# q and k split behind whole transposes, one exponential per row, one search for five blocks, junk as bytes

## The chip, the cores and the metric

The kernel runs on one core of one Trainium2 chip. The metric is the device time of one execution in microseconds (us); smaller is better. Five engines work side by side, each with its own queue that it takes in order: TensorE (PE; PEld is its weight load), VectorE (DVE), ScalarE (ACT), GpSimd (POOL) and SyncE (SP), which here only issues DMAs.

## The reference

One layer of a hybrid decoder: x is (1, 1024, 1024) float32. After an RMSNorm one projection gives everything that two attention branches of eight heads (64 wide) need. Branch A attends, for each query, to the 256 causal keys with the highest score of a light indexer; branch B to dilated windows. Cut to what the change touches:

```python
qa = rms_norm(qa.reshape(b, s, N_HEADS_A, HEAD_DIM), q_norm_a[layer])   # k, and branch B, likewise
rel = jnp.einsum('bqhd,bsd->bqhs', qib, k_idx)                          # indexer, 4 heads
score = jnp.einsum('bqhs,bqh->bqs', jax.nn.relu(rel), wb) * idx_scale
score = jnp.where(causal[None], score, -jnp.inf)
top_val, top_idx = lax.top_k(score, topk)                               # topk = 256
logits = jnp.einsum('bqhd,bqkhd->bqhk', qb, k_sel) * scale + bias
p = jax.nn.softmax(logits, axis=-1)
out = jnp.einsum('bqhk,bqkhd->bqhd', p, v_sel)
x = x + jnp.einsum('bse,ed->bsd', mixed * silu(gates), w_out[layer])
```

## The kernel before

The 1024 positions are eight blocks of 128. The 16 heads are eight **pairs** of two, taken one after the other: `ORDER` puts the four pairs of branch B first (pairs 0 to 3) and those of branch A last (pairs 4 to 7). Operands are kept as a high part of type fp32r and a low part, the rest, so that two or three fp32r matmuls stand for one exact product.

A list of timed steps sets the order in which the program is written: 64 **units** (pair, group s of 256 queries from s=3 down to 0, head h) have a slot each. In slot k stand the scores of unit k+1 (`scores`), the transposes and value matmuls of unit k (`pt`, `pv`), the projection of the next pair (`proj_item`), and a share of the two **searches** named in `CFG["sel"]`. A scheduler then places the steps on the engines' queues: a step that is ready may come ahead of one that was written earlier but isn't, and one that needs a buffer of a pool waits for a free one.

- **Projection** (L416 to L418): three matmuls for each of eight slices, two PSUM buffers. `finish` and `finish2` normalise q and k (L448, L456, L462), split k into two halves that lie side by side (L458, L459); `later` transposes these (four fp32r transposes, L471, for 256 keys) and one copy writes `kst` (L475).
- **q**: `split_q` splits q in the same way (L502, L503) for 256 queries; `transpose_q` makes two groups of four fp32r transposes (L512, L513) with a copy each (L515). `pk`, `pq` and the gate's `pg` share one PSUM buffer (tag `tr`).
- **Scores** (L537, L538): chunks of up to 512 keys; VectorE adds the bias and keeps the running maximum (L544, a custom operation and a read of its result); one exponential for each chunk (L554). The rows L live in a ring of six buffers of 512.
- **Probabilities**: transposed in f32 (L571), split by ScalarE (L575) and VectorE (L576), multiplied with the values (L587, L589). `make_gate` sums the denominators, `combine` joins and gates the result (L615 to L623).
- **Search**: the top 256 are found as a threshold, bit by bit. For one bit VectorE counts, for each block, the scores above a trial threshold (L260, whose element output `jk` is junk and takes a buffer of the ring L) and updates all thresholds (L267, L269). One such search serves blocks 2 and 3, one blocks 4 to 6; block 7 is counted by ScalarE (L309) with small updates on VectorE (L313, L315). At the end `select_mask` turns the scores into masks (L244 to L248), which the scores of branch A (pairs 4 to 7) need.

## Time and profile before

| | |
|---|---|
| median of 3 runs | 822.93 us (819.94 to 825.45) |
| profiled execution | 821.55 us |
| its span in the trace | 819.7 us, so 1.85 us lie outside |
| TensorE busy | 770.4 us, 94% |
| VectorE busy | 627.0 us, 76% |
| ScalarE busy | 525.0 us, 64% |
| GpSimd busy | 434.2 us, 53% |

Busy time is the time in which an engine had an instruction under way; shares are over the whole span, which is made of stages with different limits. TensorE's instructions overlap, so that the distance between two starts says more than the length of one. A stretch of the span is read by itself, with the wait that ends last there.

### The profile page before, as it was taken

How to read it: one execution, taken by the hardware profiler on the slowest of the kernel's cores; microseconds unless marked ns; L12 is line 12 of the kernel's file. 1: busy time of each engine (PE TensorE's matmuls, PEld its weight loads, DVE VectorE, ACT ScalarE, POOL GpSimd, SP SyncE). 2: the span in 40 equal slices, each digit the busy share in tenths (PEclk: the TensorE clock that was granted, in tenths of full speed). 3: DMA queues.
4: the chain of work that ended last, by engine and by line, in shares of the span. 5: the costliest groups of instructions: out<-in, count | busy, mean ns of one | idle time of the engine just before them, and what ended most of it. 6: DMA issues, size and time to landing. Idle time of an engine off the chain costs nothing.

```text
span 819.7 us, 13162 instructions
## 1 busy us (share of the span) xinstructions
PE 770.4 (94%) x4300; PEld 653.6 (80%) x4300; DVE 627.0 (76%) x1586; ACT 525.0 (64%) x1220; POOL 434.2 (53%) x452
## 2 busy tenths in 40 slices
...
GB/s 291 242 216 296 42 0 168 13 1 78 116 14 14 90 91 14 14 90 92 14 14 103 78 14 7 64 123 14 14 115 123 63 61 194 226 102 174 228 234 219
DMA packets 52053, 83.33 MB, mean 102 GB/s; under 512 B 5633, under 2 KB 23313, under 8 KB 51985
## 3 DMA queue, kind: packets, MB, share of 16 engines
...
q8 instruction: 34, 0.56, 0.3%
q14 instruction: 35, 0.28, 0.1%
...
## 4 chain that ended last, share of the span: by engine, by line
PE 59%; DVE 14%; ACT 3%; DMA 2%; issue 2%; POOL 1%; SPq 0%; DVEq 0%; POOLq 0%; ACTq 0%
PE pp L416 9%; PE pp L418 9%; PE pp L417 9%; PE pt L571 7%; PE po L589 6%; PE sp L537 4%; PE sp L538 4%; PE pp L644 3%; PE pp L646 3%; PE pp L645 3%; DVE jk L260 3%; DVE ptl L576 2%; DVE jk L245 1%; DVE L L544 1%; PE po L587 1%
## 5 line engine op out<-in xcount | busy, mean ns | idle before, releaser
L416 PE MATMUL pp<-wh,xh 128*128 128x512 f32 x512 | 210.0, 413 | 2.4 <-ACT praw L424 1.2
L417 PE MATMUL pp<-wl,xh 128*128 128x512 f32 x512 | 202.6, 396 | 2.6 <-POOL wl L85 2.5
L418 PE MATMUL pp<-wh,xl 128*128 128x512 f32 x512 | 202.3, 395 | 0.0
L554 ACT ACTIVATE L<-L,mn 128x512 f32<-128x512 f32 (+1 forms) x192 | 117.6, 615 | 54.0 <-DVE mn L544 52.2
L260 DVE TENSOR_SCALAR_CACHE_REDUCE jk<-sc,thr 128x512 bf16<-128x512 f32 (+4 forms) x160 | 136.3, 873 | 2.5 <-PE pt L571 2.2
L85 POOL TENSOR_TENSOR wl<-raw,wh 128x512 fp32r<-128x512 f32 x68 | 92.2, 1369 | 56.2 <-ACT wh L84 54.5
L576 DVE TENSOR_TENSOR ptl<-pt,pth 128x512 fp32r<-128x512 f32 (+1 forms) x160 | 100.2, 631 | 25.7 <-ACT pth L575 24.9
L542 POOL TENSOR_TENSOR L<-T,sc 128x512 f32<-128x512 f32 (+3 forms) x80 | 88.4, 1126 | 59.3 <-PE pt L571 42.2
L417 PEld LDWEIGHTS pp<-wl,xh 128*128 128x128 f32 x512 | 97.2, 190 | 20.2 <-POOL wl L85 4.8
L416 PEld LDWEIGHTS pp<-wh,xh 128*128 128x128 f32 x512 | 97.4, 191 | 19.4 <-ACT wh L84 2.9
L418 PEld LDWEIGHTS pp<-wh,xl 128*128 128x128 f32 x512 | 96.8, 189 | 20.1
L575 ACT CAST pth<-pt 128x512 fp32r<-128x512 f32 (+1 forms) x160 | 85.3, 541 | 37.4 <-PE pt L571 34.0
L571 PE MATMUL pt<-identr,L 128*128 128x128 f32 x576 | 89.2, 277 | 1.2 <-ACT L L554 1.0
L589 PE MATMUL po<-pth,v 128*128 128x256 f32 x256 | 73.1, 298 | 4.1 <-DVE mx L618 3.6
L589 PE MATMUL po<-ptl,v 128*128 128x256 f32 x256 | 70.6, 293 | 6.0 <-DVE ptl L576 6.0
L537 PE MATMUL sp<-kst,qt 128*128 128x512 f32 (+1 forms) x192 | 71.9, 375 | 4.3 <-DVE mn L544 4.3
L571 PEld LDWEIGHTS pt<-identr,L 128*128 128x128 f32 x576 | 66.2, 142 | 5.5 <-ACT L L554 2.4
L433 POOL TENSOR_TENSOR mu<-ss,mhalf 128x8 f32<-128x8 f32 x32 | 56.2, 1756 | 27.0 <-DVE ss L431 9.4
L84 ACT CAST wh<-raw 128x512 fp32r<-128x512 f32 x80 | 48.1, 618 | 31.3 <-DMA raw<-in_w_pair_dram 23.5
L538 PE MATMUL sp<-kst,qt 128*128 128x512 f32 (+1 forms) x192 | 67.3, 351 | 0.0
L589 PEld LDWEIGHTS po<-ptl,v 128*128 128x128 f32 x256 | 48.7, 190 | 13.9 <-DVE ptl L576 9.8
L424 ACT ACTIVATE praw<-pp,rr 128x512 f32<-128x512 f32 x64 | 43.6, 684 | 22.9 <-PE pp L418 21.2
...
## 6 DMA issues: line engine op xcount, KB each, us to landing
...
```

Source lines behind the costliest of these rows:

```text
L85: (eng or nc.gpsimd).tensor_tensor(lo, raw, f32(hi), OP.subtract)
L260: nc.vector.tensor_scalar(jk[:, :w], sc[blocks[j]], scalar, None, op, OP.add, accum_out=cnt[:, j:j + 1])
L416: pace(nc.tensor.matmul(pp, xh[tb][:, kt, :], hi, start=(kt == 0), stop=False))
L417: nc.tensor.matmul(pp, xh[tb][:, kt, :], lo, start=False, stop=False)
L418: nc.tensor.matmul(pp, xl[tb][:, kt, :], hi, start=False, stop=(kt == KT - 1))
L537: mark(nc.tensor.matmul(sp[:, :w], qt[:, h, 0, :], kk, start=True, stop=False))
L538: nc.tensor.matmul(sp[:, :w], qt[:, h, 1, :], kk, start=False, stop=True)
L542: nc.gpsimd.tensor_tensor(l[:, :w], bias, sc[qb][:, c0:c0 + w], OP.add)
L554: nc.scalar.activation(l, l, AF.Exp, bias=mn[:, done:done + 1], scale=-1.0, accum_out=blk.den[:, j, h, c:c + 1])
L571: mark(nc.tensor.transpose(t[:, si * P:(si + 1) * P], L[qb, kb // 4][:, o:o + P], identf))
L576: nc.vector.tensor_tensor(tl[:, :w], t[:, :w], f32(th[:, :w]), OP.subtract)
L589: nc.tensor.matmul(po[:, h, :], vv, t[:, 256 * j:256 * j + 256], start=(kp == 0 and j == 0 and n == 0), stop=False)
```

## The change

- **k**: the gain of k (and q) is no longer multiplied in on GpSimd but is a column (`hgain`) that scales the rows of the transposed k. k stays whole (f32, two heads side by side): two f32 transposes for 256 keys instead of four fp32r ones; then, for each head, ScalarE writes the high half and VectorE the low half (64 partitions each), out of PSUM.
- **q**: `twice_q` writes q twice side by side (GpSimd, VectorE in pairs 6 and 7); four f32 transposes for 256 queries instead of eight fp32r ones; ScalarE writes the high part, VectorE subtracts for the low part (128x512 each).
- **Rows**: L is a ring of three buffers of 1024, one for a row of a query block (for s=0 and 1 one for both blocks); one exponential for a row. The sum of two denominators and the halving of the reciprocal go; 0.5 goes into `combine`'s product.
- **Search**: blocks 2 to 6 in one search, in slots -6 to 32; its masks begin with block 6, four empty steps apart.
- **Junk**: the counts write bytes into two fixed tiles (`waste`) and take no buffer of L.

```diff
-    w=9, raw=3, praw=2, kst=3, q=4, v=5, g=5, qT=2, T=2, L=6, pt=2, s=2, proj=2, ptp=2, o=1, tr=1,
-    qhl=1, kb=1, f2=3, wpos=0, kdel=(7.5, 13, 16), gw=(7, 8, 7, 8, 8, 8, 9, 9), goff=5, lead=2, late=6,
-    outa=3, sq=0.4, qt=0.9, sel=((0, [2, 3], -8, 34), (0, [4, 5, 6], -6, 29), (1, [7], -4, 30)),
-    as_=0.5, ab=0.5, at=0.3, gpos=0.7, ahead=1, c0=4, ik=0.3, iq=0.3, is_=0.4,
+    w=9, raw=3, praw=2, kst=3, q=4, v=5, g=5, qT=1, T=2, L=3, pt=2, s=2, proj=2, ptp=2, o=1, tr=1,
+    kb=1, f2=3, wpos=0, kdel=(7.5, 13, 16), gw=(7, 8, 7, 8, 8, 8, 9, 9), goff=5, lead=2, late=6,
+    outa=3, sq=0.4, qt=0.9, sel=((0, [2, 3, 4, 5, 6], -6, 33), (1, [7], -4, 30)),
+    as_=0.5, ab=0.5, at=0.3, gpos=0.7, ahead=1, c0=4, rest=4, ik=0.3, iq=0.3, is_=0.4,
...
-            jk = scratch(BF16)
-            nc.vector.tensor_scalar(jk[:, :w], sc[blocks[j]], scalar, None, op, OP.add, accum_out=cnt[:, j:j + 1])
+            nc.vector.tensor_scalar(junk(w), sc[blocks[j]], scalar, None, op, OP.add, accum_out=cnt[:, j:j + 1])
...
-        for j in range(n):
+        for j in reversed(range(n)):
             steps.append(lambda j=j: select_mask(blocks[j], f32(thr[:, j:j + 1]), need[:, j:j + 1]))
+            steps += [lambda: None] * CFG["rest"]
...
-            nc.scalar.activation(jk[:, :w], src, AF.Sign, bias=bias, accum_out=sgn)
+            nc.scalar.activation(junk(w, 1), src, AF.Sign, bias=bias, accum_out=sgn)
...
-            kk = raw[:, :, 2:4, :]
-            gb = gk["a" if p.is_a else "b"]
-            p.eng.tensor_tensor(kk, kk, gb.unsqueeze(1).unsqueeze(1).to_broadcast([P, 2, 2, HD]), OP.mult)
...
-            p.eng.tensor_tensor(kk, kk, mu[:, :, 2:4].unsqueeze(3).to_broadcast([P, 2, 2, HD]), OP.mult)
-            k = rg.tile([P, 2, 2, P], F32R, name="k", tag="ktok", bufs=CFG["kb"])
-            nc.scalar.copy(k[:, :, :, 0:64], kk)
-            p.eng.tensor_tensor(k[:, :, :, 64:128], kk, f32(k[:, :, :, 0:64]), OP.subtract)
+            k = rg.tile([P, 2, 2, HD], F32, name="k", tag="ktok", bufs=CFG["kb"])
+            p.eng.tensor_tensor(k, raw[:, :, 2:4, :], mu[:, :, 2:4].unsqueeze(3).to_broadcast([P, 2, 2, HD]), OP.mult)
...
-            pk = ps.tile([P, 2, 2, P], F32R, name="pk", tag="tr", bufs=CFG["tr"])
+
+            pk = ps.tile([P, 2, P], F32, name="pk", tag="tr", bufs=CFG["tr"])
             for b in range(2):
-                for h in range(2):
-                    nc.tensor.transpose(pk[:, h, b, :], duo["k"][:, b, h, :], identr)
+                nc.tensor.transpose(pk[:, b, :], duo["k"][:, b].rearrange("p h d -> p (h d)"), identf)
             s, o = tb // 4, (tb % 4) * P
             if s not in p.k:
                 p.k[s] = rg.tile([P, 2, 512], F32R, name="kst", tag="kst", bufs=CFG["kst"])
-            nc.scalar.copy(p.k[s][:, :, o:o + 2 * P], f32(pk.rearrange("p h b t -> p h (b t)")))
+            pk = pk.rearrange("p b t -> p (b t)")
+            g = gk["a" if p.is_a else "b"]
+            for h, (a, b) in enumerate(((slice(0, HD), slice(HD, P)), (slice(HD, P), slice(0, HD)))):
+                ks = p.k[s][:, h, o:o + 2 * P]
+                nc.scalar.activation(ks[a], pk[a], AF.Copy, scale=g[a])
+                nc.vector.scalar_tensor_tensor(ks[b], pk[a], g[a], f32(ks[a]), OP.mult, OP.subtract)
...
-    def split_q(p, s):
+    def twice_q(p, s):
 
         q = p.q[s].rearrange("p b h d -> p (b h) d")
-        hl = sb.tile([P, 4, 192], F32R, name="qhl", tag="qhl", bufs=CFG["qhl"])
-        nc.scalar.copy(dup_hi(hl, 4), q.unsqueeze(2).to_broadcast([P, 4, 2, HD]))
-        p.eng.tensor_tensor(hl[:, :, 64:128], q, f32(hl[:, :, 0:64]), OP.subtract)
-        p.hl[2 * s] = p.hl[2 * s + 1] = hl
+        p.qd = sb.tile([P, 4, 2, HD], F32, name="qd", tag="qd", bufs=1)
+        p.eng.tensor_copy(p.qd, q.unsqueeze(2).to_broadcast([P, 4, 2, HD]))
 
     def transpose_q(p, s):
-        hl = p.hl[2 * s]
-        for qb in (2 * s + 1, 2 * s):
-            pq = ps.tile([P, 512], F32R, name="pq", tag="tr", bufs=CFG["tr"])
+
+        pq = ps.tile([P, 2, 2, P], F32, name="pq", tag="tr", bufs=CFG["tr"])
+        for b in range(2):
             for h in range(2):
-                t = hl[:, 2 * (qb % 2) + h, :]
-                nc.tensor.transpose(pq[:, (2 * h) * P:(2 * h + 1) * P], t[:, 0:128], identr)
-                nc.tensor.transpose(pq[:, (2 * h + 1) * P:(2 * h + 2) * P], t[:, 64:192], identr)
-            qt = sb.tile([P, 2, 2, P], F32R, name="qt", tag="qT", bufs=CFG["qT"])
-            nc.scalar.copy(qt.rearrange("p a b c -> p (a b c)"), f32(pq))
-            p.hl[qb] = qt
+                nc.tensor.transpose(pq[:, h, b, :], p.qd[:, 2 * b + h].rearrange("p a d -> p (a d)"), identf)
+        hi = sb.tile([P, 2, 2, P], F32R, name="qh", tag="qh", bufs=CFG["qT"])
+        lo = sb.tile([P, 2, 2, P], F32R, name="ql", tag="ql", bufs=CFG["qT"])
+        nc.scalar.copy(hi, pq)
+        nc.vector.tensor_tensor(lo, pq, f32(hi), OP.subtract)
+        p.hl[s] = hi, lo
...
+            if qb not in L:
+                t = sb.tile([P, S], F32, name="L", tag="L", bufs=CFG["L"])
+                L[qb] = t
+                if s < 2:
+                    L[qb - 1] = t[:, (qb + 1) * P:]
+            l = L[qb][:, c0:c0 + w]
             bias = p.T[h][:, col0 + c0:col0 + c0 + w]
             if p.is_a and qb >= 2:
-                nc.gpsimd.tensor_tensor(l[:, :w], bias, sc[qb][:, c0:c0 + w], OP.add)
-                bias = l[:, :w]
-            nc.vector.tensor_tensor_reduce(l[:, :w], sp[:, :w], bias, -1.0,
+                nc.gpsimd.tensor_tensor(l, bias, sc[qb][:, c0:c0 + w], OP.add)
+                bias = l
+            nc.vector.tensor_tensor_reduce(l, sp[:, :w], bias, -1.0,
                                            3e38 if done == 0 else mn[:, done - 1:done],
                                            OP.add, OP.min, mn[:, done:done + 1])
             mns[qb][1] = done + 1
-            L[qb, ci] = l
             if last:
-                j = qb - 2 * s
-                for c in range(len(chunks_of(qb))):
-                    w = min(512, nk - 512 * c)
-                    l = L[qb, c][:, :w]
-                    nc.scalar.activation(l, l, AF.Exp, bias=mn[:, done:done + 1], scale=-1.0,
-                                         accum_out=blk.den[:, j, h, c:c + 1])
+                l = L[qb][:, :nk]
+                nc.scalar.activation(l, l, AF.Exp, bias=mn[:, done:done + 1], scale=-1.0,
+                                     accum_out=blk.den[:, qb - 2 * s, h:h + 1])
...
-        if s >= 2:
-            nc.vector.tensor_tensor(blk.den[:, :, :, 0], blk.den[:, :, :, 0], blk.den[:, :, :, 1], OP.add)
         rd = sm.tile([P, 2, 2], F32, name="rd", tag="rd")
-        nc.vector.reciprocal(rd, blk.den[:, :, :, 0])
-        nc.vector.tensor_scalar(rd, rd, 0.5, None, OP.mult)
+        nc.vector.reciprocal(rd, blk.den)
...
-        nc.vector.tensor_tensor(mx, mx, pg[:, :256], OP.mult)
+        nc.vector.scalar_tensor_tensor(mx, mx, 0.5, pg[:, :256], OP.mult, OP.mult)
...
+    waste = [cp.tile([P, S], mybir.dt.int8, name=f"waste{j}") for j in range(2)]
+
+    def junk(w, j=0):
+
+        return waste[j][:, :w]
 
     def scratch(dt):
         n = 1024 if dt in (BF16, I16) else 512
         if "sb" in phase:
-            return sb.tile([P, n], dt, name="jk", tag="L", bufs=CFG["L"])
+            return sb.tile([P, S], F32, name="jk", tag="L", bufs=CFG["L"]).bitcast(dt)[:, :n]
```

How the change moves instructions, at three places. In these rows sc_89 to sc_93 are the scores of blocks 2 to 6, sc_94 of block 7; thr, cnt and rej are a search's thresholds, counts and rejections; a row-maximum is written as two rows, ISA L and ISA mn.

VectorE, among the row-maxima of the first units of pair 0, before:

```order
L260 TENSOR_SCALAR jk,cnt_250<-sc_91,thr_249 128x640
L544 ISA L,mn<-sp,T 128x384
L544 ISA mn 128x1
L260 TENSOR_SCALAR jk,cnt_250<-sc_92,thr_249 128x768
L544 ISA L,mn<-sp,T,mn 128x512
L544 ISA mn 128x1
L260 TENSOR_SCALAR jk,cnt_246<-sc_89,thr_245 128x384
L260 TENSOR_SCALAR jk,cnt_250<-sc_93,thr_249 128x896
L313 TENSOR_SCALAR arej_255<-asgn_254 128x1
L544 ISA L,mn<-sp,T 128x512
L544 ISA mn 128x1
L267 TENSOR_SCALAR rej_251<-cnt_250 128x3
```

and in the changed kernel:

```order
L543 ISA L,mn<-sp,T 128x384
L543 ISA mn 128x1
L259 TENSOR_SCALAR waste_239,cnt_242<-sc_91,thr_241 128x640
L543 ISA L,mn<-sp,T,mn 128x512
L543 ISA mn 128x1
L312 TENSOR_SCALAR arej_247<-asgn_246 128x1
L259 TENSOR_SCALAR waste_239,cnt_242<-sc_92,thr_241 128x768
L314 SCALAR_TENSOR_TENSOR abias_245<-abias_245,arej_247 128x1
L259 TENSOR_SCALAR waste_239,cnt_242<-sc_93,thr_241 128x896
L543 ISA L,mn<-sp,T 128x512
L543 ISA mn 128x1
L266 TENSOR_SCALAR rej_243<-cnt_242 128x5
```

Before, counts of two searches alternate; now the counts of one search follow each other block by block. Over the whole queue the counts (L260 before, L259 now) that stand ahead of pair 0's first row-maximum are 26 before and 9 now; between the first row-maxima of successive pairs stand 36, 36, 36 and 30 before and 62, 54, 40 and 0 now (one more stands behind pair 4's before).

VectorE, where the search for the larger blocks ends. Before, around the `need` of blocks 4 to 6 (L280), which stands in pair 3, behind the pair's first row-maxima:

```order
L260 TENSOR_SCALAR jk,cnt_246<-sc_90,thr_245 128x512
L260 TENSOR_SCALAR jk,cnt_250<-sc_93,thr_249 128x896
L544 ISA L,mn<-sp,T 128x512
L544 ISA mn 128x1
L313 TENSOR_SCALAR arej_255<-asgn_254 128x1
L267 TENSOR_SCALAR rej_247<-cnt_246 128x2
L244 TENSOR_SCALAR jk<-sc_91,thr_249 128x640
L280 TENSOR_SCALAR need_252<-cnt_250 128x3
L315 SCALAR_TENSOR_TENSOR abias_253<-abias_253,arej_255 128x1
L269 SCALAR_TENSOR_TENSOR thr_245<-rej_247,thr_245 128x2
```

and in the changed kernel around the first row-maximum of pair 3 (128x512, out of T); the only `need` (L279) stands 16 rows ahead of it:

```order
L328 TENSOR_SCALAR aneed_249<-asgn_246 128x1
L428 TENSOR_SCALAR ss<-ss 128x8
L610 SCALAR_TENSOR_TENSOR mx<-mx,pg 128x256
L570 TENSOR_TENSOR ptl<-pt,pth 128x384
L471 SCALAR_TENSOR_TENSOR kst<-pk,gkt,kst 64x256
L440 SCALAR_TENSOR_TENSOR g<-th,praw 128x256
L471 SCALAR_TENSOR_TENSOR kst<-pk,gkt,kst 64x256
L608 TENSOR_TENSOR mx<-mx,po 64x256
L609 TENSOR_TENSOR mx<-mx,po 64x256
L509 TENSOR_TENSOR ql<-pq,qh 128x512
L543 ISA L,mn<-sp,T 128x512
L543 ISA mn 128x1
```

The search now ends ahead of pair 3, and no count stands behind its first row-maximum; the masks (L244 to L248) still stand in pair 3, four of blocks 3 to 6 and that of block 7 close together behind its last row-maxima, that of block 2 in pair 4.

TensorE, a group of k and the two q groups behind it, before:

```order
L471 MATMUL pk<-identr,k 128x128 x4
L589 MATMUL po<-pth,v 128x256
L571 MATMUL pt<-identr,L 128x128 x3
L589 MATMUL po<-ptl,v 128x256
L587 MATMUL po<-pth,v 128x128
L587 MATMUL po<-ptl,v 128x128
L512 MATMUL pq<-identr,qhl 128x128
L513 MATMUL pq<-identr,qhl 128x128
L512 MATMUL pq<-identr,qhl 128x128
L513 MATMUL pq<-identr,qhl 128x128
L589 MATMUL po<-pth,v 128x256
L512 MATMUL pq<-identr,qhl 128x128
```

and in the changed kernel:

```order
L462 MATMUL pk<-identr,k 128x128 x2
L583 MATMUL po<-pth,v 128x256
L583 MATMUL po<-ptl,v 128x256
L581 MATMUL po<-pth,v 128x128
L581 MATMUL po<-ptl,v 128x128
L505 MATMUL pq<-identr,qd 128x128 x4
L531 MATMUL sp<-kst,qh 128x512 x2
L413 MATMUL pp<-wh,xh_377 128x512
L414 MATMUL pp<-wl,xh_377 128x512
```

A group of k and one of q follow each other with fewer matmuls between them; each waits for the one PSUM buffer of tag tr until the group ahead of it has been read, before by ScalarE, now by ScalarE and VectorE.

## Rows read from the trace of the kernel before

**Rows 1.** The page's first part: busy time by engine.

```profile
PE 770.4 (94%) x4300; PEld 653.6 (80%) x4300; DVE 627.0 (76%) x1586; ACT 525.0 (64%) x1220; POOL 434.2 (53%) x452
```

**Rows 2.** Windows cut at each pair's first L544, busy time by engine.

```profile
core 0: us, PE busy (x) PEld busy (x) DVE busy (x) ACT busy (x) POOL busy (x), PEclk, DMA share, GB/s
0.00:147.30 147.30, 127.37 (x623) 103.25 (x624) 97.79 (x190) 81.22 (x173) 83.06 (x85) 0.98 0.56 176
147.30:226.10 78.80, 75.19 (x437) 64.07 (x436) 71.05 (x225) 60.67 (x141) 39.48 (x45) 1.00 0.18 51
226.10:305.20 79.10, 77.25 (x455) 66.46 (x454) 75.10 (x222) 62.20 (x145) 39.31 (x45) 1.00 0.18 54
305.20:382.70 77.50, 76.48 (x450) 66.00 (x449) 71.14 (x224) 63.35 (x147) 38.48 (x45) 1.00 0.19 55
382.70:477.10 94.40, 83.92 (x461) 71.10 (x460) 90.64 (x224) 61.63 (x144) 54.05 (x50) 0.95 0.15 45
477.10:552.40 75.30, 73.36 (x433) 63.27 (x434) 52.38 (x120) 51.36 (x124) 53.78 (x58) 1.00 0.19 55
```

**Rows 3.** The same windows, L260 alone; first column after the length: VectorE's busy time.

```profile
0.00:147.30 147.30, 21.40 (x51) 0.98 0.56 176
147.30:226.10 78.80, 31.61 (x74) 1.00 0.18 51
226.10:305.20 79.10, 31.29 (x72) 1.00 0.18 54
...
382.70:477.10 94.40, 24.69 (x60) 0.95 0.15 45
```

**Rows 4.** VectorE by form, L260, and line L244 alone (ns min/median/max).

```profile
L260 DVE TENSOR_SCALAR_CACHE_REDUCE jk<-sc,thr 128x896 bf16<-128x896 f32 x32 | 36.4, 1139 | 0.0
L260 DVE TENSOR_SCALAR_CACHE_REDUCE jk<-sc,thr 128x384 bf16<-128x384 f32 x32 | 19.4, 606 | 0.2 <-PE pt L571 0.2
...
L244 DVE TENSOR_SCALAR jk<-sc,thr x5: 480/548/1575, 429.4 to 500.2; 128x640 bf16<-128x640 f32 x1, 128x768 bf16<-128x768 f32 x1, 128x896 bf16<-128x896 f32 x1, 128x384 bf16<-128x384 f32 x1
```

**Rows 5.** Groups of VectorE's instructions: busy us, mean ns of one.

```profile
L576 DVE TENSOR_TENSOR ptl<-pt,pth 128x512 fp32r<-128x512 f32 x96 | 65.4, 685 | 15.2 <-ACT pth L575 14.5
...
L617 DVE TENSOR_TENSOR mx<-mx,po 64x256 f32<-64x256 f32 x32 | 13.0, 407 | 6.9 <-ACT mx L616 4.1 <-PE sp L538 2.8
L267 DVE TENSOR_SCALAR rej<-cnt 128x2 int32<-128x2 f32 (+1 forms) x62 | 19.2, 314 | 0.2
L269 DVE SCALAR_TENSOR_TENSOR thr<-rej,thr 128x2 int32<-128x2 int32 (+1 forms) x60 | 13.9, 240 | 0.1
L605 DVE TENSOR_SCALAR rd<-rd 128x4 f32<-128x4 f32 x32 | 8.9, 279 | 0.5
L315 DVE SCALAR_TENSOR_TENSOR abias<-abias,arej 128x1 f32<-128x1 f32 x30 | 6.4, 213 | 0.0
...
L602 DVE TENSOR_TENSOR den<-den 128x4 f32<-128x4 f32 x16 | 4.3, 269 | 4.4 <-ACT L L554 4.4
```

**Rows 6.** Window of the masks, columns as in rows 2.

```profile
427.00:464.00 37.00, 30.76 (x162) 25.59 (x161) 36.84 (x66) 20.92 (x47) 28.29 (x21) 0.95 0.29 83
```

**Rows 7.** TensorE's timeline near 264 us: start us, us, instruction.

```profile
263.63 0.62 PE L571 MATMUL pt<-identr,L 128*128 128x128 f32 x4
...
264.33 0.40 PE L417 MATMUL pp<-wl,xh 128*128 128x512 f32 x1
264.56 0.40 PE L418 MATMUL pp<-wh,xl 128*128 128x512 f32 x1
...
264.92 0.22 PE L512 MATMUL pq<-identr,qhl 128*128 128x128 f32 x1
...
265.52 0.40 PE L538 MATMUL sp<-kst,qt 128*128 128x512 f32 x1
```

**Rows 8.** First score on TensorE's timeline; a window, columns as in rows 2.

```profile
125.52 0.76 PE L537 MATMUL sp<-kst,qt 128*128 128x512 f32 x1
...
127.28:147.35 20.07, 17.80 (x72) 12.82 (x71) 20.00 (x50) 9.44 (x16) 12.74 (x12) 0.97 0.47 133
```

More of the change, by code (lines that the diff above doesn't have):

```diff
@@ L47 @@
 def kernel(ctx: ExitStack, tc: tile.TileContext, xT, x, w_idx, w_pair, w_out, gain,
-                       rel_bias, onehot, lnn, qna, kna, qnb, knb, out):
+                       rel_bias, onehot, lnn, hgain, out):
     nc = tc.nc
@@ L327, in over @@
             nc.vector.tensor_scalar(thr, thr, -1.0, None, OP.mult)
-            jk = scratch(BF16)
-            nc.vector.tensor_scalar(jk[:, :w], sc[i], thr, None, OP.is_gt, OP.add, accum_out=sgn)
+            nc.vector.tensor_scalar(junk(w), sc[i], thr, None, OP.is_gt, OP.add, accum_out=sgn)
             nc.vector.tensor_scalar(need, sgn, -2.0, 2.0 * TOPK, OP.mult, OP.add)
```

34 lines of the change are left out of this document (13 added, 21 removed).

## The prediction

> **What bounds the kernel now.** The page's first part [rows 1] shows TensorE busy for 94% of the span and VectorE for 76%, which reads like a kernel that TensorE sets alone. That average mixes stages, so I cut the span at the first row-maximum (L544) of each head pair, which is the point where a pair's score work begins on VectorE, and read busy time stretch by stretch [rows 2]. The prologue lasts 147.3 us. Pairs 0 to 2 take 78.8, 79.1 and 77.5 us, with TensorE busy for 75.19, 77.25 and 76.48 of that and VectorE for 71.05, 75.10 and 71.14: the two engines are level there, and VectorE is idle for only 7.7, 4.0 and 6.4 us. Pair 3 takes 94.4 us; VectorE is busy for 90.64 of it and TensorE waits. Pair 4 takes 75.3 us with VectorE at 52.38: from there on TensorE alone sets the pace. So a microsecond of TensorE work is worth about a microsecond in pairs 4 to 7 and little in pairs 0 to 3, and a microsecond added to VectorE costs nothing in pairs 4 to 7 and nearly a microsecond in pairs 0 to 3.
>
> What fills VectorE in pairs 0 to 3 is the search: its counts (L260) take 31.61, 31.29, as much again, and 24.69 us of the four stretches and 21.40 us of the prologue [rows 3]. Each count stands there as two rows, itself and the read of its sum. One costs 31.61/37 = 0.85 us.
>
> **TensorE, part by part.** q: eight fp32r transposes and their two groups per pair and 256 queries become one group of four f32 ones. [rows 7] has both kinds without a wait: four fp32r ones begin at 264.92 and the second matmul behind them at 265.52; less one matmul's pace (264.33 to 264.56, 0.23) they take 0.37 us. Four f32 ones (the probabilities' transposes) begin at 263.63, the second matmul behind them at 264.33; the same way they take 0.47 us. So 2 x 0.37 - 0.47 = 0.27 us, times 32 = 8.6 us. k: four fp32r (0.37) become two f32 (half of 0.47), 0.13 us, times 32 = 4.3 us. Together 12.9 us off TensorE, 1.6 us for each of the eight pairs.
>
> **ScalarE and GpSimd.** The exponentials fall from 192 to 128, and the copies of k, of q's halves and of the second group of q go; GpSimd loses the k gain and two subtractions and gets a doubled copy of q. Both engines are off the pace in every stretch, so I cost this at nothing; TensorE and VectorE hide it. If that cover went, the longer exponential would delay a row's first transpose by one more chunk, a few tenths of a us at half of the units.
>
> **VectorE, part by part.** Added for each pair: four subtractions of 128x512 out of PSUM (q's low half) at 0.685, the row of the same form, and eight operations of 64x256 (k) at 0.407: 2.7 + 3.3 = 6.0 us. Removed: four halvings of the reciprocal (L605) at 0.28 and two sums of denominators (L602) at 0.27, 1.6 us; and, because one search replaces two, half of the updates, each a pair of tiny operations of 0.31 + 0.24 = 0.55 us (L267, L269) [rows 5]. Over the whole kernel that is 31 x 0.55 = 17 us off against 8 x 4.4 = 35 us on.
>
> The larger effect is one of place. The counts no longer take a buffer from the ring L, and in the program as built they stand earlier and closer. Counting the rows between the first row-maxima of successive pairs, counts before and after are: prologue 26 and 9; pair 0, 36 and 62; pair 1, 36 and 54; pair 2, 36 and 40; pair 3, 30 and 0. The search is over before pair 3 begins. VectorE takes its instructions in this order, whatever waits behind them: the row-maxima, the low halves of the probabilities and of q, on which TensorE waits, are queued behind the counts. VectorE's work by stretch is then:
> - pair 0: 71.05 + 26 x 0.85 (22.1) + 4.4 - 2 updates (1.1) + 6 updates of the ScalarE search that also come forward, at 0.21 for L315 alone (1.3) = 97.8 us;
> - pair 1: 75.10 + 18 x 0.85 (15.3) + 4.4 - 4 updates (2.2) - 0.2 = 92.4 us;
> - pair 2: 71.14 + 4 x 0.85 (3.4) + 4.4 - 7 updates (3.9) + 0.2 = 75.2 us.
>
> How long is a stretch in which VectorE has that much? In pair 1 it is busy for 95% now; in the stretch of the masks, 427 to 464 us, for 36.84 of 37 us [rows 6], 99.6%. At 97.5%, between the two, pair 0 takes 100.3 and pair 1 94.8 us. Pair 2 is level again (TensorE 76.48 - 1.6 = 74.9): 78.5 us. Sum 273.6 against 235.4 now: **+38.2 us**; at 99.6% (pair 2: 76) and 95% it is +31.6 and +44.
>
> Pair 3 loses its 30 counts, but the masks stay and one more comes ahead of pair 4: five, in one run behind the last scores of the pair, where TensorE has little other work. Bounds are pair 4's 75.3 us (masks hidden) and the 94.4 us of now; I take 87, since the masks are what remains: **-7.4 us** (-19.1 to 0).
>
> The prologue gets shorter. TensorE begins the first scores at 125.52 us, and VectorE reads them only at 147.35: from 127.28 on, when the products of the indexer are done, it is busy for 20.00 of 20.07 us [rows 8]; by the order of the queue 14 counts stand there, at 0.85 us some 12 of the 20. In the changed order only three counts (widths 512 to 768, some 0.75 to 1.0 us each), one low half of q and a few instructions on block 7's scores stand there, about 6 us. If nothing else is late, the first row-maximum comes 20 - 6 = 14 us earlier. Against that stand 8 x 0.407 = 3.3 us of k in the prologue, on a VectorE that is idle for 49 of its 147 us, and the projection for pair 1, 17.80 us of TensorE in these 20, which is still to be done, in a pair 0 that VectorE fills. I take **-11 us** (-14 to -4). In pairs 4 to 7 TensorE's saving counts in full: **-6.4 us**; the bounds are -13, twice it, if waits go too, and +3, if the one PSUM buffer that k, q and the gate share (tag tr) is held longer, since it is now freed by VectorE behind ScalarE.
>
> [...] If a count on bytes ran faster than one on bfloat16, all of this would shrink. The counts cost 606 ns for 384 elements and 1139 for 896 [rows 4], 1.04 ns an element, whereas L244, the same comparison of the same data without the sum, has a median of 548 ns with widths from 384 to 896. The row that the change keeps (a comparison with a sum) is the slow one, and nothing in the trace says that the width of the junk matters. [...]
>
> **Sum.** The profiled execution took 821.55 us, 1.85 us outside its span. 821.55 + 38.2 - 7.4 - 11 - 6.4 = 835 us. The median of the three runs is 1.4 us above that execution, so the forecast is **836 us**, rounded.
>
> **Rivals.**
> - *Pair 3 gives it back* (about 818 us). The counts are only moved; if VectorE runs without a gap in pairs 0 and 1 (+31.6) and pair 3, free of counts, falls to pair 4's 75.3 us (-19.1), then with -11 and -6.4 the sum is -4.9: 816.7, on the median 818. For it: the total of VectorE's work rises by only some 18 us. Against it: the masks, which alone fill 37 us now, and TensorE's own 83.92 us in pair 3.
> - *VectorE doesn't set the pace* (776 to 799 us), the other side. Its mechanism is the price of a count: from 0.55 us a count downwards (L244's median) VectorE has 165 x 0.3 = 50 us less, pairs 0 to 2 fall to TensorE's 75.3 - 1.6 each (-14), pair 3 to some 78 (-16), and with -6.4 and -11 it is 774, on the median 776. If counts keep their price but fit between TensorE's work after all, TensorE's 12.9 us and the prologue's 11 are what is left: 799 with the median. Against both: 7.7 us of idle time in pair 0 can't take 27 us of work.
> - *The shared PSUM buffer and the exponential chain add waits too* (about 866 us): pairs 0 to 2 at the upper bound (+44), pair 3 as now, pairs 4 to 7 at +3, -4 in the prologue: +43, 866 on the median. For it: in the new order a k group stands right ahead of a q group, and the buffer passes through ScalarE and VectorE between them; VectorE's queue is fullest there.
>
> **How the numbers follow.** Forecast 0.56, pair 3 gives it back 0.20, VectorE no bound 0.16, more waits 0.08. The time is that of the forecast. The range 808 to 860 holds the forecast's own bounds but for the far end, and the second case; it leaves out the third and most of the last. A measurement of this kernel can tell about 1% (8 us) from no change. Faster by over 1% (under 814.7) is the third case and a little of the second's lower side: 0.20; within 1% is the rest of the second and the forecast's lower side: 0.24; slower 0.56.
>
> **What the new profile would show.** Right: the first row-maximum near 136 us; pairs 0 and 1 lengthen to about 100 and 95 us with VectorE busy for 97% or more and TensorE's waits put down to VectorE; no count behind pair 3's first row-maximum; pairs 4 to 7 some 2 us shorter each. TensorE's step: groups of four q transposes at 0.47 us. Wrong: if pairs 0 to 2 stay near 78 us, the price of a count or the coupling of the two engines was misread; if a count reads 0.55 us, bytes matter; if pair 3 drops to 75 us, the masks are hidden and the second case holds.

## The result and the profile after

The changed kernel took 899.19 us, the median of 4 runs (893.44 to 1113.68), against 821.43 us: 1.0919 times as long, 95% interval 1.0838 to 1.1. The longest of the four ran with TensorE's granted clock at 0.65 in the mean (0.64 to 0.68 from stretch to stretch) and is left out of the ratio; the profile below is of a later execution of the same kernel (the first experiment), span 893.9 us against 819.7. The forecast was 836 us, range 808 to 860.

The page's first part, which answers to [rows 1]:

```profile
PE 795.1 (89%) x4108; PEld 657.6 (74%) x4108; DVE 651.3 (73%) x1552; ACT 483.0 (54%) x1028; POOL 391.8 (44%) x404
```

TensorE has 192 matmuls fewer, and its busy time is 25 us more. Windows cut at each pair's first row-maximum (L543), columns as in [rows 2]:

```profile
0.00:128.70 128.70, 110.90 (x555) 90.56 (x556) 77.13 (x147) 72.31 (x157) 70.16 (x71) 0.99 0.62 186
128.70:234.00 105.30, 95.33 (x486) 78.74 (x484) 102.64 (x294) 72.19 (x146) 42.40 (x44) 0.95 0.20 56
234.00:328.80 94.80, 84.54 (x426) 69.14 (x424) 91.81 (x253) 54.57 (x115) 32.26 (x36) 0.91 0.15 45
328.80:418.10 89.30, 81.22 (x425) 67.64 (x424) 80.94 (x231) 60.05 (x126) 32.19 (x36) 0.94 0.16 48
418.10:514.10 96.00, 82.44 (x427) 68.34 (x425) 72.68 (x133) 48.13 (x104) 44.34 (x41) 0.89 0.15 44
514.10:603.00 88.90, 79.47 (x422) 66.73 (x423) 53.89 (x121) 48.52 (x104) 50.11 (x51) 0.94 0.16 48
603.00:692.20 89.20, 79.53 (x425) 66.57 (x424) 58.53 (x127) 48.30 (x104) 43.93 (x44) 0.94 0.21 60
692.20:775.60 83.40, 77.03 (x425) 63.65 (x424) 55.59 (x128) 45.01 (x98) 45.96 (x46) 1.00 0.41 122
775.60:848.00 72.40, 66.30 (x365) 56.05 (x364) 46.25 (x102) 30.84 (x66) 24.58 (x28) 0.98 0.50 155
```

The same windows of before for the pairs that [rows 2] doesn't hold, 5 to 7:

```profile
552.40:629.30 76.90, 76.34 (x451) 65.91 (x451) 54.22 (x128) 53.79 (x129) 43.79 (x44) 1.00 0.23 69
629.30:711.60 82.30, 78.02 (x451) 67.04 (x450) 58.09 (x134) 51.54 (x126) 51.19 (x50) 0.98 0.41 125
711.60:778.20 66.60, 66.60 (x390) 57.92 (x389) 44.71 (x106) 36.65 (x90) 25.80 (x29) 1.00 0.54 170
```

Two things are to be seen. In pair 0 VectorE is busy for 102.64 of 105.3 us, 97.5% as forecast. But pairs 4 and 5, where VectorE has a third of its time free, are longer by 13.6 and 12.3 us: TensorE sits idle there for 9.4 and 9.7 us (1.9 and 0.6 before) and its granted clock is 0.94 where it was 1.00. Stretch by stretch, in us (each kernel cut at its own first row-maxima; the lower rows are the experiments' kernels):

| | prologue | 0 | 1 | 2 | 3 | 4 | 5 | 6 | 7 | tail |
|---|---|---|---|---|---|---|---|---|---|---|
| before | 147.3 | 78.8 | 79.1 | 77.5 | 94.4 | 75.3 | 76.9 | 82.3 | 66.6 | 41.5 |
| changed | 128.7 | 105.3 | 94.8 | 89.3 | 96.0 | 88.9 | 89.2 | 83.4 | 72.4 | 45.9 |
| counts untied | 136.1 | 91.2 | 82.0 | 84.2 | 86.0 | 76.4 | 76.7 | 82.5 | 66.4 | 42.5 |
| and one search | 137.1 | 88.0 | 78.1 | 76.4 | 89.5 | 79.3 | 75.5 | 80.6 | 66.0 | 41.5 |
| changed, chunked rows | 128.8 | 103.5 | 87.1 | 88.6 | 96.2 | 82.4 | 78.5 | 86.0 | 63.2 | 46.2 |
| the same, q in ptp | 129.3 | 91.8 | 79.7 | 85.6 | 90.4 | 76.6 | 74.6 | 76.9 | 67.9 | 46.0 |
| changed, q in ptp | 133.4 | 90.6 | 84.0 | 82.9 | 92.1 | 83.9 | 80.6 | 82.1 | 73.6 | 44.3 |

(`ptp` is the tag of another PSUM buffer; see experiments 9 and 13.)

The counts (L259) by window, as in [rows 3]:

```profile
0.00:128.70 128.70, 7.37 (x18) 0.99 0.62 186
128.70:234.00 105.30, 54.65 (x123) 0.95 0.20 56
234.00:328.80 94.80, 48.09 (x110) 0.91 0.15 45
328.80:418.10 89.30, 35.30 (x80) 0.94 0.16 48
```

One form of them, as in [rows 4]:

```profile
L259 DVE TENSOR_SCALAR_CACHE_REDUCE waste<-sc,thr 128x896 int8<-128x896 f32 x32 | 36.5, 1142 | 0.4
```

The counts stand where the order of the program put them, and a count on bytes costs 1142 ns where one on bfloat16 cost 1139. What is new is in TensorE's waits, summed over the span (us in total, times, longest):

```profile
PE sp L531 <- DVE mn L543: 26.8, 23, 4.1
PE pq L505 <- DVE kst L471: 17.9, 6, 5.9
PE po L583 <- DVE ptl L570: 8.0, 12, 1.2
PE sp L531 <- ACT qh L508: 7.4, 9, 1.3
```

The second line is the shared PSUM buffer (tag tr): one wait in each of the pairs 0 to 5, of 3.5, 1.8, 2.1, 5.9, 2.7 and 1.9 us. The chain of work shows the one late in pair 4, where no count is left (start us, us, piece; the last line is TensorE's timeline):

```profile
591.73 0.26 PE pk L462 x2
...
592.01 0.48 ACT kst L470
...
592.51 0.48 DVE kst L471
...
593.02 0.67 DVE k L450
593.69 1.41 DVE q L453
...
595.12 0.50 DVE kst L471
...
595.75 1.09 PE L505 MATMUL pq<-identr,qd 128*128 128x128 f32 x4 [2.71 <-DVE kst L471]
```

The q transposes stand right behind the k group and want its buffer. It is free only when two reads of ScalarE and two of VectorE are done, and each stands in its engine's own queue: here k's and q's normalisation (which runs on VectorE for pair 6) comes between VectorE's two. From the first read to the end of the last it takes 3.6 us (592.01 to 595.62). TensorE waits 2.71 us of that time, and then the four transposes take 1.09 us. The same four without a wait ahead of them, early in the same stretch, take 0.60 us, 0.36 us to the next start:

```profile
516.70 0.60 PE L505 MATMUL pq<-identr,qd 128*128 128x128 f32 x4
517.06 0.48 PE L531 MATMUL sp<-kst,qh 128*128 128x512 f32 x1
517.38 0.40 PE L532 MATMUL sp<-kst,ql 128*128 128x512 f32 x1
```

Less a matmul's pace (0.23), counted as in [rows 7], that is 517.38 - 516.70 - 0.23 = 0.45 us, where 0.47 was forecast.

The granted clock differs between the two places. Ahead of the wait it is 1.00, behind it 0.50 (windows of the same trace, columns as in [rows 2]):

```profile
585.00:590.00 5.00, 5.00 (x28) 4.19 (x27) 3.12 (x11) 2.84 (x8) 4.22 (x4) 1.00 0.37 105
595.00:600.00 5.00, 3.57 (x10) 2.72 (x11) 2.96 (x6) 0.59 (x1) 1.83 (x2) 0.50 0.00 0
```

In pair 1 counts stand in that chain, one between VectorE's two reads; ScalarE's first read of this group starts at 316.38, so that it takes 4.0 us to the end of the last, and TensorE waits 1.81 us:

```profile
316.38 0.47 ACT L470 ACTIVATE kst<-pk,gkt 64x256 fp32r<-64x256 f32 x1
...
318.20 0.49 DVE kst L471
318.69 0.02 issue
318.71 1.02 DVE waste L259 x2
...
319.83 0.50 DVE kst L471
```

The longest of the six waits, 5.89 us, is that of pair 3, where no count is left either: a mask (L246) and the sums of `combine` (L608, L609) stand between the reads, and the chain takes 7.7 us, from 498.00 to 505.71:

```profile
498.00 0.47 ACT L470 ACTIVATE kst<-pk,gkt 64x256 fp32r<-64x256 f32 x1 [0.79 <-PE pk L462]
...
503.15 1.27 DVE jk L246
504.42 0.33 DVE mx L608
...
504.76 0.42 DVE mx L609
...
505.21 0.50 DVE kst L471
```

### The profile page after: what moved, and what is told of

The parts are those of the page before. It is cut to its first block, busy times and chain, and to the rows that moved or that the text cites. A ratio compares the mean times of both kernels' runs of the same rounds, so it can differ in the third digit from the quotient of the medians.

```text
span 1111.9 us, 12452 instructions
## 1 busy us (share of the span) xinstructions
PE 1054.5 (95%) x4108; PEld 763.6 (69%) x4108; DVE 645.6 (58%) x1552; ACT 488.0 (44%) x1028; POOL 390.9 (35%) x404
## 4 chain that ended last, share of the span: by engine, by line
PE 87%; DVE 7%; ACT 2%; issue 2%; POOL 1%; SPq 0%; DMA 0%; DVEq 0%; POOLq 0%
PE pp L414 15%; PE pp L415 15%; PE pp L413 15%; PE pt L565 8%; PE po L583 7%; PE sp L531 4%; PE pp L637 4%; PE pp L635 4%; PE pp L636 4%; PE sp L532 4%; PE pq L505 2%; DVE waste L259 2%; PE pi L178 1%; DVE L L543 1%; PE pi L176 1%
## 5 line engine op out<-in xcount | busy, mean ns | idle before, releaser
L413 PE MATMUL pp<-wh,xh 128*128 128x512 f32 x512 | 269.2, 528 | 0.0
L414 PE MATMUL pp<-wl,xh 128*128 128x512 f32 x512 | 263.5, 515 | 0.0
L415 PE MATMUL pp<-wh,xl 128*128 128x512 f32 x512 | 262.8, 514 | 0.0
L570 DVE TENSOR_TENSOR ptl<-pt,pth 128x512 fp32r<-128x512 f32 (+1 forms) x160 | 100.9, 635 | 99.0 <-ACT pth L569 97.8
L259 DVE TENSOR_SCALAR_CACHE_REDUCE waste<-sc,thr 128x384 int8<-128x384 f32 (+4 forms) x160 | 139.9, 874 | 1.7
L549 ACT ACTIVATE L<-L,mn 128x1024 f32<-128x1024 f32 (+7 forms) x128 | 99.0, 774 | 56.8 <-DVE mn L543 56.5
L541 POOL TENSOR_TENSOR L<-T,sc 128x512 f32<-128x512 f32 (+3 forms) x80 | 87.4, 1120 | 100.5 <-PE pt L565 86.4
L565 PE MATMUL pt<-identr,L 128*128 128x128 f32 x576 | 117.6, 347 | 1.4 <-ACT L L549 1.4
L531 PE MATMUL sp<-kst,qh 128*128 128x512 f32 (+1 forms) x192 | 84.3, 456 | 16.8 <-DVE mn L543 11.1
L565 PEld LDWEIGHTS pt<-identr,L 128*128 128x128 f32 x576 | 83.2, 161 | 18.9 <-issue 5.6
L583 PE MATMUL po<-pth,v 128*128 128x256 f32 x256 | 92.0, 367 | 0.8 <-ACT pth L569 0.8
L532 PE MATMUL sp<-kst,ql 128*128 128x512 f32 (+1 forms) x192 | 81.8, 438 | 2.8 <-DVE ql L509 2.8
L543 DVE CUSTOM_DVE_ANT_0 L<-sp,T 128x256 f32<-128x256 f32 (+1 forms) x80 | 36.3, 461 | 68.0 <-PE sp L532 57.0
## 6 DMA issues: line engine op xcount, KB each, us to landing
skew<-rowd SPq DMA_DIRECT2D x16, 576.0 KB, 15.8
```

What stands on the lines that cost most here:

```text
L259: nc.vector.tensor_scalar(junk(w), sc[blocks[j]], scalar, None, op, OP.add, accum_out=cnt[:, j:j + 1])
L413: pace(nc.tensor.matmul(pp, xh[tb][:, kt, :], hi, start=(kt == 0), stop=False))
L414: nc.tensor.matmul(pp, xh[tb][:, kt, :], lo, start=False, stop=False)
L415: nc.tensor.matmul(pp, xl[tb][:, kt, :], hi, start=False, stop=(kt == KT - 1))
L531: mark(nc.tensor.matmul(sp[:, :w], qh[:, h, qb % 2, :], kk, start=True, stop=False))
L532: nc.tensor.matmul(sp[:, :w], ql[:, h, qb % 2, :], kk, start=False, stop=True)
```

## The experiments

Ratios are to the kernel before, measured beside each (medians 821.55 to 823.36 us), with 95% intervals. Theory V is the prediction's: VectorE's queue, filled by counts. The rivals: R, the ring L of three whole rows; W, the PSUM buffer that k, q and the gate share; S, the one search and its masks. Lines `...` in the diffs stand for lines left out.

**1. The changed kernel again** (no edit).

> The changed kernel once more, to have its stretches at the granted clock of its timed runs (0.95). Theory V (VectorE's queue, filled by counts that come early): about 898 us; pairs 0 to 2 take over 100, 95 and 80 us with VectorE at 97% or more, pairs 4 to 7 no longer than the 75.3, 76.9, 82.3 and 66.6 of before. Theory R (the ring L of three whole rows keeps the next unit's scores waiting): the loss is spread over all pairs, pairs 4 to 7 by 5 us or more each. Theory W (the one PSUM buffer of k, q and gate is held longer): the same spread, and TensorE's idle time stands ahead of the k and q transposes (L462, L505).

897.8 us. Pairs 0 and 1 are as V says, pair 2 takes 89.3 us with VectorE at 91%, but pairs 4 to 7 are 32.8 us longer in sum: V alone fails.

**2. Counts untied, alone**, on the kernel before (need shares rej's storage, to make room).

```diff
-            jk = scratch(BF16)
-            nc.vector.tensor_scalar(jk[:, :w], sc[blocks[j]], scalar, None, op, OP.add, accum_out=cnt[:, j:j + 1])
+            nc.vector.tensor_scalar(waste[:, :w], sc[blocks[j]], scalar, None, op, OP.add, accum_out=cnt[:, j:j + 1])
```

> The kernel before with one thing changed: VectorE's counts write bytes into a fixed tile and take no buffer of L. Counts ahead of the first row-maximum and in pairs 0 to 3 are then 17, 52, 42, 45 and 9 instead of 26, 36, 36, 36 and 30. Theory V: pair 0 gets 16 counts, pair 1 6, pair 2 9 more, 0.85 us each; with 90% to 95% of VectorE's time taken now, they lengthen by some 8, 3 and 8 us, and pair 3 loses up to 15: 815 to 835 us in all, 825. Theories R and W: the ring and the PSUM buffer are as before, 815 to 825 us and no stretch longer by over 4 us.

823.4 us, 1.0035 (1.0007 to 1.0063). Pairs 0 to 2 grow by 22.0 us (12.4, 2.9 and 6.7), near V's 8, 3 and 8; the prologue gives back 11.2 and pair 3 8.4. Moving the counts is nearly free.

**3. Chunked rows in the changed kernel.**

```diff
-    w=9, raw=3, praw=2, kst=3, q=4, v=5, g=5, qT=1, T=2, L=3, pt=2, s=2, proj=2, ptp=2, o=1, tr=1,
+    w=9, raw=3, praw=2, kst=3, q=4, v=5, g=5, qT=1, T=2, L=6, pt=2, s=2, proj=2, ptp=2, o=1, tr=1,
...
-                t = sb.tile([P, S], F32, name="L", tag="L", bufs=CFG["L"])
...
+            l = sb.tile([P, 512], F32, name="L", tag="L", bufs=CFG["L"])
...
```

> The changed kernel with its rows undone: L again a ring of six buffers of 512, an exponential for each chunk, two denominators and their sum; the rest as changed. Theory V: no change, 890 to 905 us (the counts stand as early as before this edit, 60, 46 and 49 in pairs 0 to 2). Theory R: most of the loss comes back, 830 to 850 us. Theory W: no change, 890 to 905 us.

861.6 us, 1.0509 (1.0457 to 1.0561): 36 us come back, less than R said; 40 stay. Of the 36, 23.8 lie in pairs 4 to 7, which hold no count. In pairs 0 to 3 the edit moves counts as well, from 62, 55, 40 and 0 to 60, 47, 50 and 2 in the traces.

**4. Counts untied and one search**, on the kernel before.

```diff
-    outa=3, sq=0.4, qt=0.9, sel=((0, [2, 3], -8, 34), (0, [4, 5, 6], -6, 29), (1, [7], -4, 30)),
-    as_=0.5, ab=0.5, at=0.3, gpos=0.7, ahead=1, c0=4, ik=0.3, iq=0.3, is_=0.4,
+    outa=3, sq=0.4, qt=0.9, sel=((0, [2, 3, 4, 5, 6], -6, 33), (1, [7], -4, 30)),
+    as_=0.5, ab=0.5, at=0.3, gpos=0.7, ahead=1, c0=4, rest=4, ik=0.3, iq=0.3, is_=0.4,
...
-        for j in range(n):
+        for j in reversed(range(n)):
             steps.append(lambda j=j: select_mask(blocks[j], f32(thr[:, j:j + 1]), need[:, j:j + 1]))
+            steps += [lambda: None] * CFG["rest"]
```

> The kernel before with VectorE's counts untied from L (as in the run that measured 823.4 us) and one search for blocks 2 to 6 with its masks as changed; q, k and rows as before. Of the 38 us between that run and the changed kernel with chunked rows (861.6), theory S gives the larger part to the search and its masks, which stand in one run ahead of pair 4: 840 to 855 us, the loss in pairs 0, 3 and 4. Theory W gives it to the split of q and k: here 820 to 830 us.

814.1 us, 0.9904 (0.9863 to 0.9945): S fails. This version takes less time than either kernel.

**5. Counts untied and the split of q and k as changed**, two searches (twice_q, transpose_q, finish2 and later of the change's diff on the kernel of 2).

```diff
-            ev.append((CFG["sq"], lambda: split_q(w.p, w.s)))
+            ev.append((CFG["sq"], lambda: twice_q(w.p, w.s)))
```

> The kernel before with VectorE's counts untied and the split of q and k as changed; two searches and chunked rows as before. Theory W (VectorE's added 4.4 us in each pair, and the one PSUM buffer of k, q and gate that VectorE now frees): 840 to 855 us, pairs 0 to 2 longer by 4 to 5 us each, TensorE waiting for kst and ql ahead of its k and q transposes in all pairs. Theory S: 820 to 830 us. By TensorE's work alone it would be 810.

861.4 us, 1.0485 (1.0425 to 1.0546), 38 us above run 2. S fails here too. The time is over W's range as well, and in pairs 0 to 3 (22.7 us of the 38) VectorE's added work isn't told apart from the buffer. In pairs 4 to 7, where VectorE has time, 10.3 us are lost. Run 3 has the same splits with one search and takes as long, 861.6 us, so the 9 us of one search don't show beside them. Pair 4 of both kernels, the untied one first, columns as in [rows 2]:

```profile
479.50:555.90 76.40, 75.87 (x449) 65.68 (x448) 53.07 (x119) 53.64 (x129) 59.20 (x63) 1.00 0.19 54
```

```profile
501.20:584.20 83.00, 77.48 (x425) 65.58 (x424) 59.57 (x131) 49.53 (x120) 47.75 (x49) 0.96 0.17 52
```

TensorE's idle time is 5.5 us instead of 0.5, and a clock of 0.96 instead of 1.00 over 83 us is worth some 3.3 us (an estimate, 0.04 of 83). With the 1.6 us that the transposes save, 5.0 + 3.3 - 1.6 = 6.7; the stretch is 6.6 us longer. For pair 5 the same sum gives 2.1 + 3.2 - 1.6 = 3.7 of 4.0.

**6 and 7. A fourth row buffer**, and its control with w=8 alone.

```diff
-    w=9, raw=3, praw=2, kst=3, q=4, v=5, g=5, qT=1, T=2, L=3, pt=2, s=2, proj=2, ptp=2, o=1, tr=1,
+    w=8, raw=3, praw=2, kst=3, q=4, v=5, g=5, qT=1, T=2, L=4, pt=2, s=2, proj=2, ptp=2, o=1, tr=1,
```

> The changed kernel with four buffers of a whole row in ring L instead of three, paid for by one buffer less in each of the weight rings (8 instead of 9; the next run has that alone). Theory R (a row's buffer comes free too late for the next unit's scores): 855 to 870 us, pairs 4 and 5 back from 89 to 80 us, the waits of 3 to 4 us ahead of a unit's scores gone. If the longer exponential is the cause and not the ring: 890 to 900.

> The changed kernel with one buffer less in each weight ring, the control of the run with four rows: no change, 893 to 905 us, by all theories, if the weights are early enough.

865.8 us, 1.0543 (1.0484 to 1.0602), and 888.3 us, 1.0805 (1.0755 to 1.0855): the fourth buffer is worth 22.5 us, R. Pairs 4 and 5 come to 86.6 and 81.2 us, less far than expected. TensorE's wait ahead of the scores, in the control and with four, is halved and not gone:

```profile
PE sp L531 <- DVE mn L543: 24.8, 22, 4.2
```

```profile
PE sp L531 <- DVE mn L543: 13.0, 13, 2.9
```

The same wait is 26.8 us in run 1 and 14.8 in run 3, but it isn't the ring's alone (18.3 us in run 11, with chunked rows). The ring itself is seen in pairs 4 to 7, where GpSimd writes the masked bias into a row of L (L541) and must wait until the transposes of the row that had the buffer are done (L565). With three whole rows (run 1), with chunks (run 3), in the control and with four rows:

```profile
POOL L L541 <- PE pt L565: 63.0, 11, 10.4
POOL L L536 <- PE pt L565: 54.1, 18, 5.2
POOL L L541 <- PE pt L565: 66.4, 11, 10.7
POOL L L541 <- PE pt L565: 32.8, 5, 10.6
```

With whole rows these waits are fewer but up to twice as long; the fourth buffer halves their sum. That the smaller weight rings alone give 9.5 us was expected by no theory.

**8. Order of the reads of k**, chunked rows.

```diff
-            for h, (a, b) in enumerate(((slice(0, HD), slice(HD, P)), (slice(HD, P), slice(0, HD)))):
+            ab = ((slice(0, HD), slice(HD, P)), (slice(HD, P), slice(0, HD)))
+            for h, (a, b) in enumerate(ab):
+                nc.scalar.activation(p.k[s][:, h, o:o + 2 * P][a], pk[a], AF.Copy, scale=g[a])
+            for h, (a, b) in enumerate(ab):
                 ks = p.k[s][:, h, o:o + 2 * P]
-                nc.scalar.activation(ks[a], pk[a], AF.Copy, scale=g[a])
                 nc.vector.scalar_tensor_tensor(ks[b], pk[a], g[a], f32(ks[a]), OP.mult, OP.subtract)
```

> The changed kernel with chunked rows (861.6 us) and the four reads of a group of transposed k in another order: ScalarE's two high halves first, then VectorE's two low halves, where now they alternate. Theory W (TensorE waits once in each pair, at the q transposes L505 right behind a k group, 2.6 to 4.3 us, until both engines have read the one buffer, and its granted clock falls behind the wait): the chain of four hands over once instead of three times, the wait shrinks by 1 us or more, 850 to 858 us. If the cost is VectorE's load alone: 858 to 865.

850.7 us, 1.0319 (1.0254 to 1.0385): 11 us less than 861.6, as W says; TensorE's waits for kst ahead of the q transposes fall from 13.5 to 5.1 us. Only 3.2 of the 11 us lie in pairs 4 to 7; in pairs 0 to 3 this edit moves counts too (60, 42, 45 and 10).

**9. q's transposes in another PSUM buffer**, chunked rows.

```diff
-        pq = ps.tile([P, 2, 2, P], F32, name="pq", tag="tr", bufs=CFG["tr"])
+        pq = ps.tile([P, 2, 2, P], F32, name="pq", tag="ptp", bufs=CFG["ptp"])
```

> The changed kernel with chunked rows, and the PSUM tile of the transposed q taken from the two buffers of the transposed probabilities (tag ptp) instead of the one that k and the gate use. Theory W: the waits ahead of L505 go, pairs 4 to 6 fall from 82.4, 78.5 and 86.0 to about 75, 75 and 81, in all 830 to 845 us. VectorE's load alone: 858 to 865, pairs 4 to 7 unchanged.

821.8 us, 0.9999 (0.997 to 1.0027): 40 us come back, more than expected. Pairs 4 and 5:

```profile
476.80:553.40 76.60, 74.53 (x411) 63.03 (x411) 57.04 (x125) 49.70 (x118) 51.21 (x54) 0.97 0.18 54
553.40:628.00 74.60, 74.47 (x428) 64.52 (x426) 55.69 (x128) 49.71 (x120) 41.08 (x39) 1.00 0.22 64
```

Pair 5 has next to no idle time left, full clock, and is 2.3 us under before; TensorE is busy for 1.9 us less. VectorE's work behind the prologue is nearly the same in both runs (576 and 570 us), so its load alone is not what these 40 us paid. But the edit also moves counts: 52, 39, 42 and 25 in pairs 0 to 3 instead of 60, 47, 50 and 2. So what the buffer itself costs in pairs 0 to 3 (28 us of the 40) and what that order costs aren't told apart; pairs 4 to 7 (14 us) hold no count. Part of the wait has only moved: TensorE now waits 7.8 us for kst ahead of scores.

**10 and 11. The split of k alone, of q alone**, each on the kernel of 4; the first piece of the diff stands for 10 (finish2, later and the gains of the change's diff), the second for 11 (twice_q and transpose_q).

```diff
+                nc.scalar.activation(ks[a], pk[a], AF.Copy, scale=g[a])
+                nc.vector.scalar_tensor_tensor(ks[b], pk[a], g[a], f32(ks[a]), OP.mult, OP.subtract)
...
+        nc.scalar.copy(hi, pq)
+        nc.vector.tensor_tensor(lo, pq, f32(hi), OP.subtract)
```

> The kernel before with counts untied and one search (814.1 us), and of the split of q and k only that of k. With both splits it takes 861.6, so 47 us are to be shared. Theory W: k holds the shared buffer through four hand-overs and q through two, so k alone costs 20 to 30 us: 834 to 844. If the cost is VectorE's load (3.3 us a pair for k, 2.7 for q): about half of it, 832 to 840, in pairs 0 to 3 only.

> The same base (814.1 us), and of the split of q and k only that of q. Theory W: the wait behind a k group is short where k is read by one copy of ScalarE; 820 to 830 us. If the cost is VectorE's load: 828 to 838, in pairs 0 to 3 only.

846.7 us, 1.0261 (1.0178 to 1.0345), and 828.2 us, 1.0054 (1.002 to 1.0089): k costs 32.6 us, more than either theory said, and q 14.1, which lies in both ranges; 46.7 together, against 47.5 for both. All of q's cost lies in pairs 0 to 3 (15.8 us; pairs 4 to 7 take 0.3 less), so that for q alone VectorE's load explains it as well as W. Of k's, 32.5 us lie there and 3.7 in pairs 4 to 7, and 7.1 come back in the prologue.

**12. Whole rows with an exponential for each chunk.**

```diff
...
-                l = L[qb][:, :nk]
...
+                for c in range(len(chunks_of(qb))):
+                    l = L[qb][:, 512 * c:min(512 * c + 512, nk)]
...
```

> The changed kernel with rows in three whole buffers as changed, but an exponential for each chunk of 512 behind the row's maximum, and the two denominators summed. Theory R (the ring): no change, 892 to 908 us. If the longer exponential costs: towards the 861.6 us of the chunked ring, 865 to 880.

894.6 us, 1.0855 (1.0785 to 1.0924): the longer exponential costs nothing that these runs can tell; the ring does.

**13 and 14. The changed kernel with q in ptp**, then with the edit of run 6 too.

```diff
-        pq = ps.tile([P, 2, 2, P], F32, name="pq", tag="tr", bufs=CFG["tr"])
+        pq = ps.tile([P, 2, 2, P], F32, name="pq", tag="ptp", bufs=CFG["ptp"])
```

> The changed kernel with the PSUM tile of the transposed q in the buffers of tag ptp; rows as changed. If the two losses add: 898 less the 40 us that this edit gave with chunked rows, 855 to 865 us. If the ring's loss comes only with the late q: 820 to 835.

> The same with four buffers of a row and weight rings of 8 (which took the changed kernel from 897.8 to 865.8 us). If the losses add: 825 to 840 us. If they are one: 815 to 825.

850.2 us, 1.0309 (1.0253 to 1.0365), under the range for losses that add and over the other, and 827.8 us, 1.0045 (1.0019 to 1.0071; its weight rings of 8 have a part in it that wasn't measured here). With q in another buffer the whole rows still cost 28 us, with q in the shared one 36: two losses, mostly side by side.

**15. The edits of 8 and 9 together**, on the kernel of 3 (the diffs stand there).

> Chunked rows, q's tile in ptp (821.8 us with that alone) and ScalarE's two halves of k ahead of VectorE's two. k's chain still holds the buffer that the gate uses; with fewer hand-overs 814 to 822 us; by VectorE's load, which stays, no less than 814.

824.5 us, 1.0002 (0.9976 to 1.0029): nothing on top of 9, where up to 8 us were expected.

## Why the prediction was wrong

The direction was right, the time some 62 us short. The forecast's terms against run 1, in us:

| | forecast | run 1 |
|---|---|---|
| pairs 0 to 2 | +38.2 | +54.0 |
| pair 3 | -7.4 | +1.6 |
| prologue | -11 | -18.6 |
| pairs 4 to 7 | -6.4 | +32.8 |
| tail | none | +4.4 |

- **The step that failed first** is "In pairs 4 to 7 TensorE's saving counts in full: -6.4 us", 39 of the 61 us between the columns. These pairs take 301.1 us before and 333.9 in run 1. With chunked rows they take 310.1 (run 3), and with q in another PSUM buffer too 296.1 (run 9): the whole rows cost 23.8 us there and the shared buffer 14.0, and in the other order it is 13.6 for the buffer and 24.2 for the rows (run 13: 320.3). Without both waits the saving is there, 5.0 us where 6.4 stood.
- **The shared buffer** stood in the text, as the bound of +3 and in a rival of 0.08, with no row behind its size. The +3 us were 0.75 us a pair. What counts is that four reads of two engines form a chain, each behind what its engine has queued, while TensorE stands behind the q transposes: in one pair without counts 3.6 us, of which TensorE waits 2.7, and 7.7 and 5.9 us where the masks stand between. Taking q out of that buffer gave back 40 of the 47.5 us that the split costs, in pairs 0 to 3 together with another order of the counts.
- **A step that was missing**: L as three whole rows. "I cost this at nothing" looked only at the longer exponential, which run 12 shows to cost nothing that can be told. Three buffers of 1024 hold as many bytes as six of 512, and yet cost 36 us, 22.5 of which a fourth buffer gives back. A row now comes free only as a whole: in pairs 4 to 7 GpSimd waits up to 10.4 us for one where it waited up to 5.2 for a chunk, and VectorE's row-maxima wait for GpSimd in turn (5.5 us in sum, 2.8 with chunks). For pairs 0 to 3 (10 of the 36 us) no trace shows this, and there the edit moved counts as well.
- **Both waits cost twice**, which no step had: TensorE's granted clock is 0.94 in pairs 4 and 5 (run 1) where it was 1.00; with chunked rows it is 0.96 and 1.00 (run 3), with the split alone and chunked rows 0.96 in both (run 5). The clock's share of pair 4's loss in run 5 is, by the estimate there, some 3.3 of 6.6 us.
- **VectorE's work** was read well in share and a little low in size: 102.64 us in pair 0 at 97.5% of it (97.8 and 97.5% forecast), 91.81 in pair 1 (92.4), 80.94 in pair 2 (75.2). Pair 1 took 94.8 us, as forecast, and pair 0 105.3 instead of 100.3; how much of pair 1's time is luck isn't known, since with chunked rows (run 3) it takes 87.1 us but holds 47 counts instead of 55. Pair 2 took 89.3 instead of 78.5 with VectorE at 91%. Pair 3, at 96.0 instead of 87, had 72.68 us of VectorE's work and 13.6 us of idle TensorE, 5.9 of them the one wait for the shared buffer.
- **"The larger effect is one of place"** fell as a net effect. Untied counts alone lengthen pairs 0 to 2 by 22.0 us and cost 2 to 3 in all; the prologue was worth -18.6 where -11 stood (-14 to -4). The rival by which pair 3 gives it back comes near run 2 in kind (-8.4 there, -11.2 in the prologue), for this part of the change.
- **One search** was a gain of 9 us from run 2 to run 4, where the forecast took only its updates off VectorE, 7.2 us in pairs 0 to 2. Beside the split of q and k (runs 3 and 5) no gain is left.
- **Bytes.** The count's price did not change, as the forecast took it to: 1142 ns for 128x896 with bytes as its output, 1139 with bfloat16.

So the 76 us of run 1 come, by runs 2, 4, 3 and 1 in turn, as +2 (counts untied), -9 (one search and its masks), +47 (q and k, 40 of it undone by another PSUM buffer) and +36 (whole rows). Some terms depend on the order: by runs 2, 5, 3 and 1 they are +2, +38 (q and k), 0 (one search) and +36. In run 4 ScalarE's junk still took a buffer of L, for want of room, unlike in run 3.
